# Holding a reload back until the fourth group is raised, in a fused LoRA kernel on one core

## The chip, the core and the metric

The kernel runs on one core of a Trainium2 chip. The core has five engines that run their own instruction streams and meet only through semaphores: TensorE (PE, with its weight loads shown as PEld), VectorE (DVE), ScalarE (ACT), GpSimd (POOL) and SyncE (SP). Here SyncE issues every DMA. The metric is the device time of one execution in microseconds, as the median of several runs; smaller is better. Before the change it is 123.69 us (three runs, 123.66 to 123.69).

## What is computed

```python
# x: 16 x 512 x 768, A: 768 x 16, B: 16 x 768, all float32; scale = 0.5
def reference(x, A, B, scale):
    lora = np.matmul(np.matmul(x, A), B)
    return (x + scale * lora).astype(np.float32)
```

Seen as rows, x is 8192 x 768. Every row is read once, gets a rank-16 correction, and is written once: 25.2 MB in and 25.2 MB out.

## The kernel before

**Tiles and groups.** The 8192 rows are 64 tiles of 128 rows. Eight tiles make a group, so there are eight groups, called g0 to g7 here; the change's "fourth group" is g3. A load of one group, or a store of one group, moves 3072 KB. The rows stay in SBUF in one buffer, `x_sb`, with room for 48 tiles (six groups). The last two groups, g6 and g7, therefore have to go where g0 and g1 were (`tiles` takes the tile number modulo 48, L103).

**Loads and stores.** `LOADS` (L106) has eight entries. I number them 0 to 7: loads 0 and 1 bring g0, loads 2, 3 and 4 bring g1, g2 and g3, load 5 brings g4 and g5 together (6144 KB), load 6 brings g6 and load 7 brings g7. `STORES` (L128) has five: store 0 is g0, store 1 is g1, and stores 2, 3 and 4 are g2+g3, g4+g5 and g6+g7 (6144 KB each). Load 6 overwrites the space of g0, so it must wait until store 0 has landed (`s_out0`); load 7 overwrites that of g1 and must wait for store 1 (`s_out1`).

**One group's way through the engines.** ACT and POOL each cast half of a group's rows to float16 into `xn` (L194). DVE turns the 32x32 blocks of `xn` into `xt` (L250). PE projects with A into `ps_yt` (24 matmuls, L281), ACT scales and spreads the result into `y_bd` (four instructions, L238), and PE raises it with B, pair of tiles by pair of tiles, into two PSUM buffers `lora_ps` (four matmuls a pair, L302; the code calls this `raised`). DVE adds each pair onto `x_sb` in place (L255), and then the rows can be stored. There are four pairs in a group (`PAIRS` is 4).

**What is counted where.** Every raised pair adds one to `s_lora` at its last matmul (L310), so `s_lora` reaches 10 after the second pair of g2 and 16 after the last pair of g3. DVE frees a PSUM buffer through `s_free` (L259). For the last pair of a group that ends a store it counts `s_sum` instead, and SyncE passes the release on to PE (`e.sem_inc`, L144) when it gets to that point in its own stream. `s_raise` (L307) counts the groups whose raising has begun.

**SyncE's stream around the change.** SyncE works strictly in order. After loads 0 to 5 it waits for the sums of g0 and of g1, then until `s_lora` is 10 (L169), and issues stores 0 and 1. It waits for store 0 to land (L172) and issues load 6 (L173); waits for store 1 to land (L174) and issues load 7 (L175). Then, for each of stores 2, 3 and 4, it waits for the sum, passes the PSUM release on, and issues the store; store 2 waits in addition until the sixth group's raising has begun (L181). All transfers go through one DMA queue.

Of the kernel before, what the change touches and what calls it, by code (L numbers as in the profile page):

```python
# [28 lines left out]
def kernel(  # L29
# [20 lines left out]
    PAIRS = GROUP // 2  # L50
# [32 lines left out]
    def sem(name):  # L83
        sems.append(nc.alloc_semaphore(name))
        return sems[-1]
# [10 lines left out]
    def memory(t2, i, s, n):  # L96
        S = PARTS[i]
        return t2[ds(parts[i], S * P), :].rearrange("(p s) d -> p s d", s=S)[:, ds(s, n), :]

    def held(i, s, n):  # L100
        return tiles(where.index((i, s)), n)
# [18 lines left out]
    s_y, s_spread, s_lora = sem("s_y"), sem("s_spread"), sem("s_lora")  # L120
# [14 lines left out]
    def on_sync(e):  # L135
        def load(k):
            ld = LOADS[k]
            e.dma_start(out=held(*ld), in_=memory(x2, *ld)).then_inc(s_load[k], 16)  # L138

        def summed(k):  # L140
            e.wait_ge(s_sum, k + 1)
            if STORED[k] + 1 < NG:

                e.sem_inc(s_free[PAIRS - 1], 1)  # L144

        def store(k, done):
            st = STORES[k]
            e.dma_start(out=memory(out2, *st), in_=held(*st)).then_inc(done, 16)

        load(0)  # L150
        load(1)
        e.wait_ge(s_ready, 1)
        blocks = A.rearrange("(c e) r -> c (e r)", e=64)
        for c in range(SETS):
            e.dma_start(
                out=a_rows[c : SET * SET : SET, :], in_=blocks[ds(c * SET, SET), :]
            ).then_inc(s_a, 16)
        e.wait_ge(s_brows, 1)
        e.dma_start(out=b_rows[0 : R * APART : APART, :], in_=B).then_inc(s_b, 16)
        for k in range(2, len(LOADS) - 2):  # L160
            load(k)

        for p in range(2, PAIRS):
            e.sem_inc(s_free[p], 1)
        summed(0)
        summed(1)


        e.wait_ge(s_lora, 2 * PAIRS + 2)  # L169
        store(0, s_out0)  # L170
        store(1, s_out1)
        e.wait_ge(s_out0, 16)  # L172
        load(len(LOADS) - 2)  # L173
        e.wait_ge(s_out1, 16)  # L174
        load(len(LOADS) - 1)  # L175
        for k in range(2, len(STORES)):
            summed(k)
            if k == 2:


                e.wait_ge(s_raise, 6)  # L181
            store(k, s_out)
# [90 lines left out]
    def on_tensor(e):  # L273
# [58 lines left out]
        for p in range(PAIRS):  # L332
            raised(p)

    on_sync(nc.sync)
    on_gpsimd(nc.gpsimd)
    on_scalar(nc.scalar)
# [46 lines left out]
```

## Time and profile before

| | |
|---|---|
| time, median of three runs | 123.69 us (123.66 to 123.69) |
| span of the profiled execution, first to last instruction | 121.9 us |
| difference of the two: start and end of the program around the span | 1.8 us |
| bytes moved by DMA | 50.43 MB, at 414 GB/s over the span |
| busiest engine | DVE, 81.7 us (67%) |

The profiled execution's own time is given as its span alone; the median of the unprofiled runs stands 1.8 us above it. In the profile an instruction is named by its line in the kernel, its engine, and the tile that it writes and reads. A DMA issue on SyncE is short (about 0.3 us); the transfer itself goes on in 16 DMA engines, and the profile gives the time from the issue to the landing, which is when the semaphore is complete. The profile also cuts the span in 40 slices of 3.05 us and shows the busy share of each engine, and of the DMA engines, in each. The PE clock that was granted is full in all slices up to 97.6 us.

### The profile page before, as it was taken

How to read it: one execution, taken by the hardware profiler on the slowest of the kernel's cores; microseconds unless marked ns; L12 is line 12 of the kernel's file. 1: busy time of each engine (PE TensorE's matmuls, PEld its weight loads, DVE VectorE, ACT ScalarE, POOL GpSimd, SP SyncE). 2: the span in 40 equal slices, each digit the busy share in tenths (PEclk: the TensorE clock that was granted, in tenths of full speed). 3: DMA queues.
4: the chain of work that ended last, by engine and by line, in shares of the span. 5: the costliest groups of instructions: out<-in, count | busy, mean ns of one | idle time of the engine just before them, and what ended most of it. 6: DMA issues, size and time to landing. Idle time of an engine off the chain costs nothing.

```text
span 121.9 us, 885 instructions
## 1 busy us (share of the span) xinstructions
PE 50.5 (41%) x322; PEld 29.3 (24%) x322; DVE 81.7 (67%) x42; ACT 37.4 (31%) x43; POOL 28.4 (23%) x24
## 2 busy tenths in 40 slices
PE   0000239487457457647756714774674320000000
PEld 0000026244233233424424402442442110000000
DVE  0003850799999999999999959999995991000000
ACT  4003929444426402917230093643004000000000
POOL 7732638044026002607100090630000000000000
PEclk9999999999999999999999999999999985555555
DMA  3999999999997996999989999998998999899890
GB/s 67 421 429 429 443 443 403 451 435 419 476 516 339 435 516 298 460 403 443 443 363 460 427 427 468 451 484 387 419 500 387 403 516 403 371 516 419 355 516 0
DMA packets 1928, 50.43 MB, mean 414 GB/s; under 512 B 236, under 2 KB 236, under 8 KB 392
## 3 DMA queue, kind: packets, MB, share of 16 engines
q1 hardware_dynamic: 1928, 50.43, 96.8%
HBM read 25.26 MB, written 25.17 MB: 414 GB/s over the span
## 4 chain that ended last, share of the span: by engine, by line
DVE 33%; DMA 29%; PE 9%; ACT 6%; POOL 2%; issue 2%; SPq 0%; DVEq 0%
DVE x_sb L255 21%; DMA x_sb<-in_x_dram 20%; DVE xt L250 12%; DMA out_dram<-x_sb 9%; PE ps_yt L281 6%; ACT xn L194 3%; PE lora_ps L302 3%; ACT y_bd L238 2%; POOL xn L194 2%; SPq L138 0%; SPq L379 0%; DVEq L268 0%; SPq L133 0%
## 5 line engine op out<-in xcount | busy, mean ns | idle before, releaser
L255 DVE TENSOR_TENSOR x_sb<-x_sb,lora_ps 128x1536 f32<-128x1536 f32 x32 | 53.7, 1735 | 1.4 <-PE lora_ps L302 1.4
L302 PE MATMUL lora_ps<-b_mm,y_bd 128*128 128x512 f16 (+1 forms) x128 | 25.1, 328 | 23.7 <-ACT y_bd L238 15.3
L194 ACT CAST xn<-x_sb 128x3072 f16<-128x3072 f32 (+1 forms) x9 | 23.4, 2609 | 37.2 <-DMA x_sb<-in_x_dram 28.0
L250 DVE STREAM_TRANSPOSE xt<-xn 128x3072 f32<-128x3072 f32 (+1 forms) x9 | 27.0, 3005 | 6.7 <-PE ps_yt L281 4.9
L194 POOL CAST xn<-x_sb 128x3072 f16<-128x3072 f32 (+1 forms) x8 | 20.7, 2588 | 45.3 <-DMA x_sb<-in_x_dram 28.6
L281 PE MATMUL ps_yt<-xt,w_bd 128*128 128x256 f16 x192 | 25.7, 285 | 11.9 <-DVE xt L250 11.9
L281 PEld LDWEIGHTS ps_yt<-xt,w_bd 128*128 128x128 f16 x192 | 18.7, 100 | 19.6 <-issue 15.0
L302 PEld LDWEIGHTS lora_ps<-b_mm,y_bd 128*128 128x128 f16 x128 | 10.5, 97 | 36.8 <-ACT y_bd L238 17.5
L238 ACT ACTIVATE y_bd<-ps_yt 32x256 f16<-32x256 f32 x32 | 12.0, 374 | 17.7 <-PE ps_yt L281 17.4
L243 DVE STREAM_TRANSPOSE a_t<-a_rows 32x1024 f32<-32x1024 f32 x1 | 1.9, 1945 | 11.2 <-DMA a_rows<-in_A_dram 11.2
L315 PE MATMUL lora_ps<-b_half,pick 128*128 128x512 f16 (+1 forms) x2 | 0.8, 500 | 12.5 <-POOL b_half L212 12.5
L315 PEld LDWEIGHTS lora_ps<-b_half,pick 128*128 128x128 f16 x2 | 0.1, 105 | 12.5 <-issue 12.5
L220 POOL COPY w_bd<-w_one 32x384 f16<-32x384 f16 x4 | 2.0, 501 | 0.2
L212 POOL CAST b_half<-b_rows 128x768 f16<-128x768 f32 x1 | 0.8, 830 | 4.5 <-DMA b_rows<-in_B_dram 4.5
L194 ACT ACT_TABLE_LOAD x1 | 1.3, 1283 | 0.9 <-SPq L133 0.9
L202 POOL MEMSET w_bd<- 128x1536 f32 x1 | 1.4, 1372 | 0.0
L199 POOL MEMSET a_rows<- 32x1024 f32 x1 | 0.9, 941 | 0.5 <-SPq L133 0.5
L214 POOL CAST w_one<-a_t 32x384 f16<-32x384 f32 x1 | 0.8, 847 | 0.9 <-DVE a_t L243 0.9
L231 ACT CAST b_mm<-lora_ps 128x768 f16<-128x768 f32 x1 | 0.8, 798 | 0.0
L200 POOL MEMSET b_rows<- 128x768 f32 x1 | 0.7, 727 | 0.0
L203 POOL MEMSET y_bd<- 128x512 f32 x1 | 0.5, 514 | 0.0
L205 POOL TENSOR_SCALAR_AFFINE_SELECT pick<-pick 128x128 f16<-128x128 f16 x1 | 0.3, 300 | 0.0
(5 smaller groups left out, 0.6 us busy)
## 6 DMA issues: line engine op xcount, KB each, us to landing
out_dram<-x_sb SPq DMA_DIRECT2D x3, 6144.0 KB, 20.0
x_sb<-in_x_dram SPq DMA_DIRECT2D x5, 3072.0 KB, 14.8
x_sb<-in_x_dram SPq DMA_DIRECT2D x1, 6144.0 KB, 41.9
out_dram<-x_sb SPq DMA_DIRECT2D x2, 3072.0 KB, 14.9
x_sb<-in_x_dram SPq DMA_DIRECT2D x1, 2304.0 KB, 9.7
x_sb<-in_x_dram SPq DMA_DIRECT2D x1, 768.0 KB, 4.5
a_rows<-in_A_dram SPq DMA_DIRECT2D x3, 16.0 KB
b_rows<-in_B_dram SPq DMA_DIRECT2D x1, 48.0 KB, 7.4
```

Source lines behind the costliest of these rows:

```text
L194: ins = copy(out=xn[:, ds(first, n), :], in_=tiles(t, n))
L199: e.memset(a_rows[0:Q], 0.0).then_inc(s_ready, 1)
L202: e.memset(w_bd.rearrange("p c k m -> p (c k m)").bitcast(fp32), 0.0)
L212: e.tensor_copy(out=b_half, in_=b_rows).then_inc(s_bh, 1)
L220: e.tensor_copy(out=w_bd[ds(b * Q, Q), :, :, ds(b * Q, R)], in_=w_one).then_inc(s_w, 1)
L238: last = e.mul(out=y_bd[q, :, q], in_=y_ps[q, :, :], mul=sc)
L243: e.transpose(out=a_t[0:Q].rearrange("i k r c -> i (k r) c"), in_=a_rows[0:Q].rearrange("c (i k r) -> c (k r) i", k=2, r=R),).then_inc(s_r ...
L250: return e.transpose(out=ts[0], in_=ts[1])
L255: ins = e.tensor_tensor(out=xs, in0=xs, in1=lora[p % 2], op=mybir.AluOpType.add)
L281: mm = e.matmul(y_ps, w_bd[:, c, k, :], xv[:, :, c, :, k], start=(m == 0), stop=(m == MMS - 1),)
L302: mms.append(e.matmul(t[:, k, ds(n0, w)], y_bd[:, 2 * p + k, :], b_mm[:, ds(n0, w)], start=True, stop=True,))
L315: last = e.matmul(lora[0][:, 0, ds(n0, w)], pick.rearrange("p b r -> p (b r)"), b_half[:, ds(n0, w)], start=True, stop=True,)
```

## The change

SyncE waits for one thing more before it issues load 6: after store 0 has landed, it also waits until `s_lora` has reached 16, that is until PE has raised the last pair of g3. Nothing else in the program differs; every other instruction keeps its place on its engine.

```diff
         store(0, s_out0)
         store(1, s_out1)
         e.wait_ge(s_out0, 16)
+        e.wait_ge(s_lora, 4 * PAIRS)
         load(len(LOADS) - 2)
         e.wait_ge(s_out1, 16)
         load(len(LOADS) - 1)
```

From the added line on, line numbers of the changed kernel are one higher than those of the kernel before.

## The prediction

> **What bounds the kernel now.** I began with the page's busy shares, its 40 slices and its table of DMA queues.
>
> ```profile
> span 121.9 us, 885 instructions
> PE 50.5 (41%) x322; PEld 29.3 (24%) x322; DVE 81.7 (67%) x42; ACT 37.4 (31%) x43; POOL 28.4 (23%) x24
> ...
> DMA  3999999999997996999989999998998999899890
> ...
> q1 hardware_dynamic: 1928, 50.43, 96.8%
> ```
>
> No engine is full, but the 16 DMA engines are: 96.8% of the whole span in one queue, with no slice below 6 tenths between the first and the last (a transfer's packets are counted where they begin, so single slices are uneven). So the end is set by when the queue starts, how many bytes it has to carry, and whether it ever runs dry. The chain of waits, read next, says the same for the stretch in question, although its shares give DVE the first place (a chain may follow either side where two finish close together):
>
> ```profile
> 42.42 1.49 PE lora_ps L302 x8
> 43.92 11.36 DMA out_dram<-x_sb
> 55.30 14.76 DMA x_sb<-in_x_dram
> 70.11 2.76 POOL xn L194
> ```
>
> Store 0 is issued at 43.92 us and lands at 55.28; load 6 is issued at 55.30 and lands 14.76 us later, at 70.06. Why 14.76 us for 3072 KB? The timelines of SyncE, ACT and POOL, cut to the landings, tell what one such transfer takes by itself. They hold the issues first (start, duration), then the casts that waited for a load:
>
> ```profile
> 43.92 0.82 SPq L148 DMA_DIRECT2D out_dram<-x_sb  x2
> 55.30 0.34 SPq L138 DMA_DIRECT2D x_sb<-in_x_dram  x1
> 62.70 0.34 SPq L138 DMA_DIRECT2D x_sb<-in_x_dram  x1
> 74.87 0.34 SPq L148 DMA_DIRECT2D out_dram<-x_sb  x1
> ...
> 18.57 2.75 ACT L194 CAST xn<-x_sb 128x3072 f16<-128x3072 f32 x1 [2.52 <-DMA x_sb<-in_x_dram]
> 48.02 2.75 ACT L194 CAST xn<-x_sb 128x3072 f16<-128x3072 f32 x1 [5.66 <-DMA x_sb<-in_x_dram]
> 70.08 2.75 ACT L194 CAST xn<-x_sb 128x3072 f16<-128x3072 f32 x1 [7.88 <-DMA x_sb<-in_x_dram]
> 77.40 2.75 ACT L194 CAST xn<-x_sb 128x3072 f16<-128x3072 f32 x1 [3.01 <-DMA x_sb<-in_x_dram]
> ```
>
> Each cast or issue begins some 0.02 us behind its landing. Load 5 is there at 48.02, store 0 at 55.30, store 1 at 62.70 (SyncE's next issue waited for it), load 6 at 70.08, load 7 at 77.40. The steps are 7.28, 7.40, 7.38 and 7.32 us: one transfer after the other, in the order of issue, each at the full rate (3.146 MB in 7.32 us is 430 GB/s). Load 6, issued at 55.30, thus lay behind store 1 until about 62.7 and took its own 7.4 us only then. This is the reading on which the forecast rests: the 4th line of the chain is half a wait in the queue.
>
> **The added wait.** It ends with the last pair of g3. The row of that pair on PE:
>
> ```profile
> 58.47 0.82 PE L302 MATMUL lora_ps<-b_mm,y_bd 128*128 128x512 f16 x4 [0.84 <-DVE x_sb L255]
> ```
>
> The group's four matmuls end at 58.47 + 0.82 = 59.29. The signal to SyncE takes little: the second pair of g2 ends the PE piece 42.42 + 1.49 = 43.91 in the chain above, and store 0 is issued at 43.92. So load 6 is issued at about 59.32, in place of 55.30: 4.0 us later. The wait is real; it is not yet met when store 0 lands. It can't stop the program either: g3's raising needs load 5's landing, PE's own order and DVE's releases, nothing that SyncE does after this point.
>
> **What those 4.0 us cost.** Store 1 still has the queue until about 62.70. The load is issued 62.70 - 59.32 = 3.4 us before that. Does 3.4 us cover the time between an issue and the first byte? Two rows bound it.
>
> ```profile
> x_sb<-in_x_dram SPq DMA_DIRECT2D x1, 768.0 KB, 4.5
> out_dram<-x_sb SPq DMA_DIRECT2D x3, 6144.0 KB, 20.0
> ...
> 76.00:90.00 14.00, 8.64 (x59) 5.19 (x60) 14.00 (x9) 4.25 (x5) 2.75 (x1) 1.00 1.05 453
> ```
>
> Load 0, the first one, meets an empty queue: 4.5 us for 768 KB, of which the bytes at the rate above are a quarter of 7.32, 1.8 us. That leaves 2.7 us for everything before the first and after the last byte together. With it, load 6 by itself would land at 59.32 + 2.7 + 7.3 = 69.3, still 0.8 us before the 70.08 that the queue allows anyway. The other row is nearer, a transfer in the running queue: store 2 is issued at 74.87, 2.5 us before load 7 lands at 77.40, and the stretch from 76 to 90 (last two columns: share of the DMA engines, GB/s) shows them full, 1.05 and 453 GB/s. A lead of 2.5 us leaves no hole, and here it is 3.4 us. So I take zero, and the work that hides the 4.0 us is store 1; without that cover the cost would be up to 4.0 us, all of it at the end, since a queue that is full to the end never makes it up.
>
> The Trainium skill speaks against a late issue: DMA: Bandwidth & Descriptors, section "Rules for kernel authors", says to issue a DMA early and wait late so that its fixed setup overlaps with other work. Its section "Anatomy of one DMA — SWDGE (gpsimd) path" gives about 2.0 us plus bytes / 436e3 (a fit for GpSimd's path; this queue is the hardware one); an estimate from it lands load 6 alone at 59.32 + 2.0 + 7.2 = 68.5 us, before 70.08, so by its figures the rule would cost nothing here.
>
> **What is queued behind the waiting SyncE.** Load 7 waits for store 1 anyway (62.70). After it comes the PSUM release that SyncE passes on, for which PE waited in the waits (total, times, longest):
>
> ```profile
> SPq L138 <- DMA out_dram<-x_sb: 17.6, 2, 10.5
> PEld lora_ps L302 <- SPq L144: 0.5, 1, 0.5
> ```
>
> SyncE's two waits for stores are 10.5 and 7.1 us. The second shrinks to about 62.68 - 59.66 = 3.0 us and ends when it ended before, so load 7, the release at 63.1 and PE's 0.5 us stay. They would move only if `s_lora` reached 16 after some 62.3 us; there are 3.0 us to spare. Store 2 is tied to load 6 through ACT's cast of g6, which stands ahead of g5's y_bd on ACT: 70.08 to the issue at 74.87 is 4.8 us, and load 7 lands 7.3 us after load 6 whatever happens, so the 2.5 us of lead go along with it. DVE, PE, ACT and POOL keep their order and get their data when they did.
>
> **What is left: the change of direction.** Between store 1 and load 6 the queue goes from writing to reading. From 55.30 to 70.08 two transfers took 14.78 us. Twice 7.32 would be 14.64. The smallest step here comes from the tail: store 4 is issued at
>
> ```profile
> 101.04 0.33 SPq L148 DMA_DIRECT2D out_dram<-x_sb  x1
> ```
>
> and lands 20.0 us on (the median of three is this one: store 2 and store 3 lie on either side of it), at 121.0; the three stores from 77.40 to 121.0 are six times 3072 KB at 7.27. Twice 7.27 is 14.54. So 0.14 to 0.24 us are lost about this turn, with load 6 queued 7.4 us ahead. If a late issue avoids that, the gain is up to 0.24. The turn from load 5 to store 0 is the row nearest to the new situation: the stores are issued 4.1 us before load 5 lands, near the 3.4 of load 6. From load 2's landing, 18.57, to 48.02 stand 29.45 us for four times 3072 KB; four times 7.32 or 7.27 are 29.28 or 29.08, so 0.17 to 0.37 us were lost with that lead. Between -0.24 and +0.37 (the whole of that loss put on top) I take 0, since the nearest row's 0.17 to 0.37 and the present 0.14 to 0.24 overlap: the loss stays, whichever side of it varies.
>
> **Sum.** Wait 4.0 us, hidden 4.0; turn 0. The span stays 121.9, and the time is 121.9 plus the 1.8 us that the median shows around it: 123.7 us.
>
> **The rivals.** (1) Faster: a load that lies long in the queue disturbs the store ahead of it, and a shorter lead cures it. For it: 7.40 and 7.38 are the longest steps, and the later turn from load 7 to store 2, issued only 2.5 us ahead, is not to be seen in the 7.32. Against it: that turn goes the other way, and the lead of 4.1 us before store 0 had a loss all the same. Time: 123.69 - 0.24 = 123.45, or a little lower if the last DMA engine gains more than the mean.
> (2) Slower: the new load's descriptors reach the DMA engines while they finish store 1, and hold the last packets up, as load 5's end seems to have been. It costs 0.17 to 0.37 on top and decides from 0.25: 123.9 to 124.1.
> (3) Slower, the cover is too short: the engines that finish store 1 first run dry before load 6 is there. It begins where issue to first byte exceeds 3.4 us less the spread of the engines. The row of store 2 speaks against it; if the first byte came 4 us behind the issue, the hole would be 0.6 us, 124.3.
> (4) Load 6 already moved bytes during store 1, so that holding it loses a head start. Store 1's 7.40 us against 7.28 for store 0 leaves 0.12 us for that at most, and store 1 would win what load 6 loses: no change.
>
> **How the numbers follow.** About 0.2% (0.25 us) is what a measurement of this kernel can tell from no change. My forecast, with rival 4: 0.54, its own range 123.45 to 123.93. Rival 1: 0.22. Rival 2: 0.16. Rival 3: 0.08. That gives faster 0.22, same 0.54, slower 0.24. With cases of both signs the range reaches from rival 1's lower side, 123.35, to the upper end of rival 2 and a little into 3, 124.15; outside lie most of rival 3 and the far ends of the others, 2 in 10.
>
> **What would show it.** SyncE's issue of load 6 at about 59.3, the next at 62.7; its waits split into 10.5 for store 0, 4.0 for PE and 3.0 for store 1. ACT's casts that waited for loads 6 and 7 at 70.1 and 77.4, store 2 issued at 74.9, the DMA share in the slices from 58 to 70 us as full as now. Rival 1 would show as a sum below 14.6 us from store 0's landing to load 6's; rivals 2 and 3 as one above 15.0, rival 3 with a slice of fewer GB/s just behind 62 us. The forecast is wrong if load 6 lands more than 0.25 us away from 70.1, or if the three stores behind 77.4 change their pace, which nothing in this change touches.

## The result, and the profile after

The changed kernel is slower: 124.25 us against 123.66 us, a ratio of 1.0058 (95% interval 1.0038 to 1.0079). The ratios in this document are not the quotients of the two medians, and they leave out runs more than 1.5% above the fastest of the same kernel (one of the changed kernel's later runs and four of one experiment). The runs also scatter: nine of them lie between 123.77 and 125.25 us, where the nine of the kernel before lie between 123.44 and 123.75. The profile is of the slowest of the nine, 125.25 us with a span of 123.4, so it shows the loss in full.

Its page, in the same rows as above:

```profile
span 123.4 us, 886 instructions
PE 52.0 (42%) x322; PEld 30.3 (25%) x322; DVE 81.8 (66%) x42; ACT 37.5 (30%) x43; POOL 28.4 (23%) x24
...
PEclk9999999999999999999999985599999975555555
DMA  3999999999999799999999996996996999899790
...
q1 hardware_dynamic: 1928, 50.43, 95.9%
```

The bytes are the same, the engines' busy times nearly so, and the DMA queue's share fell from 96.8% of 121.9 us to 95.9% of 123.4. The chain of waits has a new length at the changed place:

```profile
59.49 0.02 SPq L173
59.51 0.05 issue
59.56 12.08 DMA x_sb<-in_x_dram
71.63 0.02 issue
71.66 2.75 ACT xn L195
...
76.02 2.74 PE lora_ps L303 x8
```

Load 6 is issued at 59.56, as worked out (59.32 there), but it lands at 71.63 in place of 70.06. That is 1.57 us later, about the whole of the 1.5 us that the span grew. SyncE's timeline and waits say that nothing else moved ahead of it by more than 0.3 us (the 14.6 us are the wait for store 0 and the added wait in one):

```profile
59.56 3.34 SPq L138 DMA_DIRECT2D x_sb<-in_x_dram  x2
76.66 26.45 SPq L148 DMA_DIRECT2D out_dram<-x_sb  x3
...
SPq L173 <- PE lora_ps L303: 14.6, 1, 14.6
SPq L138 <- DMA out_dram<-x_sb: 2.7, 1, 2.7
```

The two loads are issued in the 3.34 us from 59.56, so load 7 goes out at about 62.56 as before (62.70). Store 1 was on time. Yet load 6 needed 12.1 us, of which 7.3 are its bytes. Where the other 4.8 us went can be read from the trace's records of single DMA packets. A load of one group is 128 packets of 24 KB, eight for each of the 16 DMA engines; a packet normally takes 912 ns, and each engine takes its packets back to back. The records do not name the engine; I joined each packet to the one that ended just before it began. Here is the turn from store 1 to load 6 for four of the 16 (start in us + duration in ns; the bar stands between the two transfers):

```
changed kernel, load 6 issued at 59.56
engine a   60.06+912  60.97+912 | 61.88+912  62.79+912  63.70+912  64.61+912
engine b   60.47+912 | 61.38+1204  62.59+994  63.57+909  64.48+912
engine c   60.12+912  61.03+912 | (1.75 idle)  63.69+1227  64.92+912
engine d   60.90+912 | (1.76 idle)  63.58+928  64.50+912
```

Fourteen engines went on at once, some with slow first packets. Two stood still for 3.5 us together (which of the two late starts is whose can't be told, so it may also be 1.63 and 1.88): their first packets of load 6 began 4.0 and 4.1 us after the issue. They were not the first to come free. They ended store 1 at 61.81 and 61.94, some 2.3 us behind the issue, while the engines that came free first, from 61.14 on, went on without a hole. A load has landed when its last engine has. By the semaphore's sixteen counts, 14 engines had load 6 done between 69.04 and 70.24 us, and the two late ones at 71.19 and 71.63.

The rest follows from the last of them. ACT casts g6 at 71.66, PE raises g5 at 76.02, and store 2 goes out at 76.66 instead of 74.87. The engines that were on time had finished load 7 by then, so the queue had a second gap (DMA share and GB/s in the last two columns, from 76.2 to 77.5 us, before and after):

```profile
76.20:77.50 1.30, 1.01 (x10) 0.89 (x11) 1.30 (x2) 0.10 (x1) 0.07 (x1) 1.00 1.05 454
```

```profile
76.20:77.50 1.30, 1.30 (x5) 0.60 (x4) 1.30 (x1) 0.00 (x0) 0.00 (x0) 0.50 0.18 76
```

Fifteen engines stood idle here, between 0.2 and 1.7 us. Whether that second gap costs anything is asked below.

### The profile page after: what moved, and what is told of

The parts are those of the page before. It is cut to its first block, busy times and chain, and to the rows that moved or that the text cites. A ratio compares the mean times of both kernels' runs of the same rounds, so it can differ in the third digit from the quotient of the medians.

```text
span 123.4 us, 886 instructions
## 1 busy us (share of the span) xinstructions
PE 52.0 (42%) x322; PEld 30.3 (25%) x322; DVE 81.8 (66%) x42; ACT 37.5 (30%) x43; POOL 28.4 (23%) x24
## 3 DMA queue, kind: packets, MB, share of 16 engines
q1 hardware_dynamic: 1928, 50.43, 95.9%
## 4 chain that ended last, share of the span: by engine, by line
DVE 42%; DMA 18%; PE 11%; ACT 8%; issue 3%; SPq 0%
DVE x_sb L256 27%; DMA x_sb<-in_x_dram 18%; DVE xt L251 15%; PE ps_yt L282 7%; ACT xn L195 6%; PE lora_ps L303 5%; ACT y_bd L239 2%; SPq L138 0%; SPq L380 0%; SPq L133 0%; SPq L173 0%
## 5 line engine op out<-in xcount | busy, mean ns | idle before, releaser
L303 PE MATMUL lora_ps<-b_mm,y_bd 128*128 128x512 f16 (+1 forms) x128 | 26.2, 340 | 24.1 <-ACT y_bd L239 16.7
L282 PE MATMUL ps_yt<-xt,w_bd 128*128 128x256 f16 x192 | 26.5, 291 | 11.6 <-DVE xt L251 11.6
L282 PEld LDWEIGHTS ps_yt<-xt,w_bd 128*128 128x128 f16 x192 | 19.3, 103 | 19.7 <-issue 14.7
```

Of the source, the lines that this page charges most:

```text
L282: mm = e.matmul(y_ps, w_bd[:, c, k, :], xv[:, :, c, :, k], start=(m == 0), stop=(m == MMS - 1),)
L303: mms.append(e.matmul(t[:, k, ds(n0, w)], y_bd[:, 2 * p + k, :], b_mm[:, ds(n0, w)], start=True, stop=True,))
```

## The experiments

My theory after seeing this (A): a load needs several microseconds from its issue until every DMA engine has begun it without a stumble; with a short lead a few engines begin late, and the latest one sets the end. The rivals were that the wait itself or SyncE's order costs (B), that the load must be in the queue from the beginning of store 1 (C), and that the second gap, not the first, is what costs.

**The wait without the delay.** The count that is asked for is met before store 0 lands.

```diff
         e.wait_ge(s_out0, 16)
+        e.wait_ge(s_lora, 4 * PAIRS - 2)
         load(len(LOADS) - 2)
```

> The added wait asks for two pairs of g3 in place of four, which PE has raised at about 53.9 us, before store 0 lands at 55.3. The wait is in the program but is met already, and load 6 goes out at 55.3 as in the kernel before. Theory A (the late issue lets some DMA engines start load 6 late): no holes, 123.5 to 123.8 us, the narrow spread of the kernel before. Theory B (the wait instruction as such costs, or the order on SyncE): as slow as the changed kernel, 123.8 to 125.3.

Measured: 123.49 us (123.39 to 123.84), ratio 0.9997 (0.9982 to 1.0013). B falls: the instruction and its place cost nothing that shows.

**A smaller delay.** One pair less than in the change.

```diff
         e.wait_ge(s_out0, 16)
+        e.wait_ge(s_lora, 4 * PAIRS - 1)
         load(len(LOADS) - 2)
```

> The wait asks for three pairs of g3: load 6 goes out at about 57.7 us, 5 us before store 1 lands, where the changed kernel has 3.0 and the kernel before 7.4. Theory A with a start-up of up to some 4 us on single DMA engines: the lead now covers it, 123.5 to 123.9 us and load 6 landed by about 70.1. Theory C (not the lead, but that the load is not in the queue when store 1 begins to move): slow and scattered like the changed kernel, 123.8 to 125.3, load 6 landed at up to 71.6.

Measured: 123.59 us (123.38 to 123.88), ratio 1.0000 (0.9987 to 1.0014). The chain and ACT's cast of g6 in its profile:

```profile
58.00 11.75 DMA x_sb<-in_x_dram
...
69.77 2.75 ACT L195 CAST xn<-x_sb 128x3072 f16<-128x3072 f32 x1 [7.30 <-DMA x_sb<-in_x_dram]
```

A delay of 2.7 us is hidden completely, and no engine stood idle at the turn. C falls. This also answers the hope that a shorter time in the queue would gain something: it doesn't.

**A delay until the queue is empty.**

```diff
         e.wait_ge(s_out0, 16)
+        e.wait_ge(s_lora, 4 * PAIRS + 1)
         load(len(LOADS) - 2)
```

> The wait asks for the first pair of g4, raised at about 63.1 us, after store 1 has landed (62.6): load 6 goes out into an empty queue. Theory A: every DMA engine has a hole, from its end of store 1 (61.2 to 62.2) to about 0.9 us behind the issue, 64.0 (the 0.9 us is what store 2 took in the changed kernel, issued at 76.66 into idle DMA engines), so 1.8 to 2.8 us on all: 125.4 to 126.4 us, with a narrow spread, since all engines start together and none waits behind a store. If single DMA engines take up to 4 us from issue to start whatever else runs, it is 127 to 128 and scattered.

Measured: 127.38 us (126.82 to 127.66), ratio 1.0293 (1.0253 to 1.0333). The direction and the narrow spread are as expected, the size is not. It falls where the other theory put it (127 to 128), but not for its reason, since no engine took 4 us from the issue. SyncE issues both loads together, and the stretch behind store 1 is empty (share 0.02, 8 GB/s):

```profile
63.46 0.82 SPq L138 DMA_DIRECT2D x_sb<-in_x_dram  x2
...
61.20:64.20 3.00, 0.82 (x4) 0.31 (x4) 3.00 (x2) 1.25 (x4) 0.00 (x0) 1.00 0.02 8
```

By the packets, the engines began load 6 between 64.43 and 65.15 us, 1.0 to 1.7 us behind the issue, and their first packets took 1.35 to 2.0 us in place of 0.91. The sixteen holes come to 48.8 engine-microseconds and the slow packets to 10.8; (48.8 + 10.8) / 16 = 3.7 us, against the measured 127.38 - 123.50 = 3.9 (3.6 by the ratio). I had left out the slow first packets, and had taken the start-up from a store (0.9 us).

**The second gap taken away.** The changed kernel, but store 2 no longer waits for the raising of g5.

```diff
+        e.wait_ge(s_lora, 4 * PAIRS)
         load(len(LOADS) - 2)
...
-                e.wait_ge(s_raise, 6)
```

> The changed kernel without SyncE's wait for the sixth group's raising ahead of store 2, so that store 2 lies in the queue from about 63 us on. In the profiled run of the changed kernel 14 of the 16 DMA engines stood idle between 76.1 and 77.6 us because store 2 was issued late (76.66). Theory A1 (the two DMA engines that lost 1.6 to 1.9 us ahead of load 6 set the end, the holes before store 2 cost nothing more): as slow and scattered as the changed kernel, 123.8 to 125.3. Theory A2 (the holes before store 2 are what costs): back at 123.5 to 123.9.

Measured: 124.73 us (124.27 to 125.87), ratio 1.0119 (1.0061 to 1.0178). It isn't faster, so A2 falls: taking the second gap away did not bring the time back. The profile of the changed kernel agrees. After the second gap the other engines end together at 121.2 to 121.5 us, and the last packets end later than that, at 122.05 and 122.20. But this run's own profile, of the fastest of its four executions (124.27 us), has no late engine:

```profile
59.09 4.25 SPq L138 DMA_DIRECT2D x_sb<-in_x_dram  x2
...
70.28 2.75 ACT L195 CAST xn<-x_sb 128x3072 f16<-128x3072 f32 x1 [8.39 <-DMA x_sb<-in_x_dram]
78.07 2.75 ACT L195 CAST xn<-x_sb 128x3072 f16<-128x3072 f32 x1 [3.48 <-DMA x_sb<-in_x_dram]
```

Load 6 is there at 70.28, nearly as before, and load 7 lands 7.8 us after it instead of 7.3. The control that comes next has store 2 early without the added wait, and its load 7 takes 7.8 us too, so that part is a cost of the early store. The ratios of the two are the fair comparison: 1.0016 (1.0000 to 1.0033) there against 1.0119 (1.0061 to 1.0178) here. So the added wait costs even where store 2 isn't late. Whether a late engine did it in the three longer executions of this run was not seen, since they have no profile.

**The changed kernel once more, and the control for store 2.** The second of these is the kernel before with the wait for the raising of g5 removed.

> The changed kernel once more, beside the other kernels of this call. 123.8 to 125.3 us, scattered. If theory A holds, a profile of it shows single DMA engines that begin load 6 late, and its time goes with the latest of them: load 6 landed at 70.1 us makes about 123.7, load 6 landed at 71.6 about 125.2.

> The kernel before without the wait for the sixth group's raising ahead of store 2, which then lies in the queue from about 63 us on, behind load 7. It is the control for the run with both edits (124.3 to 125.9 us), whose profile showed every DMA engine's last packets of load 7 slow (up to 0.5 us each) with store 2 queued behind them. If that queueing costs by itself: 123.9 to 124.4. If the queue alone decides and a transfer that lies in it is harmless: 123.4 to 123.8.

The changed kernel measured 123.89 us this time (123.57 to 125.49), ratio 1.0024 (1.0001 to 1.0047). Of both sets, 19 executions, nine lie between 123.57 and 123.91 and six above 124.7: the harm comes in some executions only. The profiled one (124.86) again has a late engine. It stood idle for 0.9 us from 61.7, began load 6 some 2.7 us behind the issue, and landed it at 70.99, the other fifteen by 70.22:

```profile
59.90 11.09 DMA x_sb<-in_x_dram
...
71.01 2.75 ACT L195 CAST xn<-x_sb 128x3072 f16<-128x3072 f32 x1 [8.30 <-DMA x_sb<-in_x_dram]
```

Both profiles of the changed kernel are of long executions; that the short ones have no late engine is inferred, not seen.

The control measured 123.87 us (123.53 to 124.33), ratio 1.0016 (1.0000 to 1.0033), between the two ranges I gave, so a cost of about 0.2 us is likely but hardly clear of none. Its packets have a cause for one: with store 2 in the queue from 62.9 on, the end of load 7 has 6.8 engine-microseconds of slow packets at 74 to 76 us, up to 0.76 us each, where the kernel before has none.

**Between the two leads.** The wait for three pairs, and a short count on SyncE after it.

```diff
         e.wait_ge(s_out0, 16)
+        e.wait_ge(s_lora, 4 * PAIRS - 1)
+        for _ in range(16):
+            e.sem_inc(s_pad, 1)
         load(len(LOADS) - 2)
```

> Load 6 between the two leads tried so far: SyncE waits for three pairs of g3 (met at about 57.7 to 58.0 us) and then counts a semaphore of its own 16 times before it issues the load, at 58.4 to 59.2 us by the estimate that one count takes 0.03 to 0.08 us. Issued at 58.0 the time was that of the kernel before, issued at 59.5 it was 123.6 to 125.5. A threshold that is a start-up time of single DMA engines: in between, a median of 123.6 to 124.0 and some runs above 124. If the wait for the fourth pair as such mattered (what PE does then), and not the time of the issue: 123.4 to 123.8, all runs.

Measured: 123.79 us (123.58 to 123.98), ratio 1.0020 (1.0008 to 1.0032), with the issue at 58.53. No execution is above 124, so the expectation was met in the median only. The rival, that the wait for the fourth pair matters as such, asked for 123.4 to 123.8 in all runs; four of the ten are above that, and the ratio is clear of 1, which speaks against it but not strongly. In one table, from the profiles (idle and slow are engine-microseconds from 60 to 66 us, worked out from the packets; the last column is the ratio of the runs):

| load 6 issued | first engine ends store 1 | idle | slow packets | load 6 landed, first to last engine | ratio |
|---|---|---|---|---|---|
| 55.30 (before) | 61.47 | 0.1 | 4.3 | 69.08 to 70.06 | 1 |
| 58.00 | 61.06 | 0 | 1.2 | 68.80 to 69.75 | 1.0000 |
| 58.53 | 61.22 | 0.3 | 1.2 | 68.93 to 70.29 | 1.0020 |
| 59.09 (store 2 early) | 61.23 | 0.3 | 1.7 | 69.13 to 70.26 | 1.0119, both edits |
| 59.56 (after) | 61.14 | 3.5 | 5.1 | 69.04 to 71.63 | 1.0058 |
| 59.90 (after, again) | 61.14 | 1.5 | 9.1 | 69.29 to 70.99 | 1.0024 |
| 63.46 | 61.17 | 48.8 | 10.8 | 72.65 to 73.57 | 1.0293 |

A lead of 3.1 us before the first engine comes free is free of cost, 2.7 is at the edge, and 1.2 to 1.6 let single engines begin late in the executions profiled. With 2.1 the one profile shows none, so it is also a matter of chance. The slow packets are not all of one kind: in the kernel before, 3.5 of the 4.3 are last packets of store 1, with load 6 queued behind it.

**Is it the load, or what lies ahead of it?** Four runs with a short lead at other places. A store behind a store, twice:

```diff
         store(0, s_out0)
+        e.wait_ge(s_raise, 4)
         store(1, s_out1)
```

> A store behind a store, with a short lead: store 1 waits until g3's raising has begun (about 52.6 us), 1.4 us before the first DMA engine ends store 0; load 6 goes out at 55.3 as in the kernel before. Theory D (what arrives at a DMA engine that is writing to memory arrives late, whatever it is): holes of up to 2.5 us on single engines about 54 to 57 us, 123.8 to 125.5 and scattered. Theory E (it is the load, whose read has to come through behind the stores): no holes, 123.4 to 123.8.

> Once more the store behind a store with a lead of about 1 us. The first run had a profile without a hole or a slow packet at 53 to 57 us, and yet ten times with a median of 124.16 us (123.88 to 124.61), of which the profiled execution was the fastest. Theory E: again no hole about 54 us; if the 0.5 us are real, the profile shows them elsewhere, by the landings at 55.3, 62.6, 70.0, 77.4 us and the end. Theory D: single engines with holes about 54 us in a slower execution.

Store 1 was issued at 52.90 and 53.24, 0.8 and 0.5 us before the first engine ended store 0. No engine was late in the first profile, and four stood idle for up to 0.36 us in the second; in neither is a packet there slow by much more than 0.04 us. So a store began within about 0.9 us, and D falls. Even so both were slower: 124.16 us, ratio 1.0049 (1.0029 to 1.0068), and 124.32 us, ratio 1.0069 (1.0044 to 1.0094). The second profile shows where: store 1 landed at 62.88, 7.8 us behind store 0 and not 7.4, and the turn to load 6, which had been issued at 55.10, has slow packets on all sixteen engines (11 engine-microseconds, 0.7 us each). The first profile has 7 there. Most of both are last packets of store 1, of the kind seen in the kernel before, and no engine is late. In the second that is (11 - 4.3) / 16 = 0.4 us an engine more than the kernel before has at this turn, with a full lead and without a late engine; why, I can't say.

A load behind a load, with two leads. The release for PE is passed on ahead of the wait.

```diff
         e.wait_ge(s_out1, 16)
+        summed(2)
+        e.wait_ge(s_lora, 4 * PAIRS + 3)
         load(len(LOADS) - 1)
```

> A load behind a load, with a short lead: load 7 waits until the third pair of g4 is raised (about 67.55 us), 1.2 us before the first DMA engine ends load 6 and 2.5 before load 6 has landed; the release for PE is passed on ahead of that wait. An empty queue began a load 1.0 to 1.7 us behind its issue, so holes of up to 0.5 us on the first engines come in any case and cost little, since the first engines end first. Theories D and E (stores that are still going on are needed for the long delay): 123.4 to 123.9. Theory F (single engines begin any load up to 4 us late when they are busy): holes up to 2.5 us, 123.9 to 125.5.

For the second lead, the added wait asks for `s_taken` at 6 instead.

> Load behind load with a lead near 3 us: load 7 waits until PE has begun to project g5 (about 65.5 us), 3 us before the first DMA engine ends load 6; the run before this one issued it at 68.0 and had it start 1.0 to 2.1 us later with first packets of 1.15 to 2.0 us in place of 0.91. Theory E (a load wants some 3 us of lead, whatever lies ahead of it): no holes, normal packets, 123.4 to 123.8 us. If a lead of 3 us is enough only behind stores: 123.9 to 125.

In the first, PE was later than I had worked out, and load 7 went out at 68.04, only half a microsecond before the first engine came free. It began 1.0 to 2.1 us behind the issue, and its first packets took 1.15 to 2.0 us:

```profile
68.04 0.34 SPq L138 DMA_DIRECT2D x_sb<-in_x_dram  x1
...
69.54 2.75 ACT L197 CAST xn<-x_sb 128x3072 f16<-128x3072 f32 x1 [6.88 <-DMA x_sb<-in_x_dram]
79.87 2.75 ACT L197 CAST xn<-x_sb 128x3072 f16<-128x3072 f32 x1 [6.02 <-DMA x_sb<-in_x_dram]
```

From load 6 to load 7 it took 10.3 us, not 7.3. This profile is of one of the kernel's longest executions (126.04 us), so I use it for the start-up only; all ten lie between 123.77 and 126.19 us, with a median of 125.02, and the ratio, without the four longest, is 1.0070 (1.0034 to 1.0105). The lead was too short to decide between D, E and F: such a start would be late in any case. In the second, load 7 was issued at 66.17, 2.4 us before the first engine came free: 123.67 us, ratio 1.0002 (0.9985 to 1.0019), no hole there above 0.1 us, and two slow packets. So a load needs more lead than a store: behind a load 0.5 us was too little and 2.4 was enough, behind a store 1.2 to 1.6 was too little and 3.1 was enough. A single engine that begins up to 4 us late was seen behind a store only.

## Why the prediction was wrong

- **The queue as the bound, and transfers in order of issue: right.** The span grew by what the last engine lost (1.5 against 1.57 us), and a queue that ran empty for 3 us cost 3.6 to 3.9. (What I call the 4th line of the chain is the 3rd, at 55.30.)
- **When the wait ends, and what is queued behind SyncE: right.** 59.56 instead of 59.32; load 7 and the release stayed within 0.15 us.
- **"So I take zero, and the work that hides the 4.0 us is store 1": here it failed.** The term of the sum that was wrong is "hidden 4.0": of the delay of 4.3 us, 1.57 came through to the landing in the profiled execution, and about 0.6 to the median time (0.3 in the second set of runs). Two rows carried it. The row that I called nearest was store 2, issued 2.5 us ahead, without a hole behind it. But that is a store, and a store began within about 0.9 us of its issue, while the late engines began the load after 2.7 to 4.1 us. The other row was load 0, 2.7 us for everything except its bytes, which left 0.8 us to spare. On the late engine of load 6 the same sum came to 12.1 - 7.3 = 4.8 us. The lead was counted wrongly as well: 3.4 us to the landing of store 1, when its first engine was free 1.6 us behind the issue and the two that were late some 2.3. Counted to the first free engine (76.01), store 2 had not 2.5 us but 1.1.
- **Rival 3 was the right one, with a chance of 0.08.** It said that engines would run dry if the first byte came 4 us behind the issue, and gave 124.3 us. Two engines began 4.0 and 4.1 us behind it, and the median is 124.25. That the numbers agree so well is luck: the hole doesn't come on all engines, 0.6 us long, but on one or two in some executions, longer, which fits the scatter; the second set of runs had a median of 123.89. The range ended at 124.15 because I trusted the row of store 2 too far.
- **"The 2.5 us of lead go along with it": wrong in the mechanism, without a cost.** The lead of store 2 depends on the last engine of load 6, while its deadline depends on the first engine of load 7. Fifteen engines stood idle, but in that profile they ended before the late two all the same.
- **The turn taken as 0: right.** Rival 1's disturbance is real: with load 6 queued early the last packets of store 1 are slow, and issued at 58.00 fewer are (1.2 engine-microseconds at the turn in place of 4.3). But the time was the same, so there was nothing to gain and rival 1 falls. Rival 2, slow last packets of store 1, isn't what the packets of the changed kernel show: the last packets of store 1 took 912 to 926 ns, and the slow and late ones belong to load 6.
- **The rule that spoke against the change was right.** I put beside the sum that the Trainium skill (DMA: Bandwidth & Descriptors, "Rules for kernel authors") wants a DMA issued early, so that its fixed setup is covered. The runs agree: what lies between issue and first packet was covered at 58.0 and not, on every engine, at 59.6. The Trainium skill's figure of 2.0 us from its anatomy of a DMA, which it gives for GpSimd's path, is below the 4.8 us of the late engine here.

What stays open is what the late engines wait for. The trace shows no packet on them between store 1 and their start, and doesn't say whether the descriptors or the first read came late. The same page of the Trainium skill, under "Latency and other measured facts", gives 2 us for an access to HBM at high load; no run here measured that alone.

## What to carry to other kernels

Count the lead of a queued transfer from its issue to the moments when the DMA engines come free, not to the landing of the transfer ahead, which came 1.4 us after the first free engine here. Bound its start-up by a row of the same kind: here a load behind a store began without a hole with 3.1 us of lead, and a store with about 1. One late engine of sixteen delays the whole transfer, so a cover that holds on average is not yet a cover. Scatter that appears with a change can be a sign that a margin has become too small.

## What the runs showed of the hardware that I had not expected

- A load and a store differ in their start. Into idle engines, store 2 of the changed kernel began 0.9 us behind its issue; load 6 in the empty queue began after 1.0 to 1.7 us, and its first packets took half as long again or more.
- Lying in the queue for long isn't harmless everywhere. With store 2 queued 12 us ahead behind load 7, that load's last packets took up to 0.76 us longer each; with store 2 issued at 74.87, as in the kernel before, none did.
- The granted PE clock fell to half (0.50 in the row from 76.20 above) where PE had stood idle for 5.3 us before g5's raising, and eight matmuls there took 2.74 us:

```profile
72.00:76.00 4.00, 0.00 (x0) 0.00 (x0) 1.46 (x1) 3.91 (x5) 2.43 (x1) 0.61 0.99 424
```

The third figure from the end is the clock. The run with the wait already met shows the same fall from 76.0 us on (0.50) and is as fast as the kernel before, so the fall alone does not explain the loss.
